# From the last differential head on, SyncE's transfers in written order, with strips and output weights moved and two casts reordered

## The chip, the cores and the metric

The kernel runs on one core of a Trainium2 chip. The metric is the device time of one execution in microseconds, taken as the median of several runs. Before the change the median is 902.08 us (three runs, 901.36 to 903.22).

## The reference: what is computed

One macaron block over 512 tokens of width 1024, in float32: half a SwiGLU feed-forward layer, a token mixer, another half feed-forward layer, a final RMS norm. The mixer is where the change lies. It has four differential heads (two softmax maps each, the second subtracted with a weight lambda, then an RMS norm of the head's output) and eight dilated heads. Cut to what matters:

```python
proj = h @ w_in
qa, ka, va, qb, kb, vb = jnp.split(proj, [...], axis=-1)
# 4 differential heads
s = q_blk @ k.T * scale + bias          # causal, -inf above the diagonal
p = softmax(s); a = p[0] - lam * p[1]
oa = rmsnorm(a @ v, subln_gain) * (1 - lam0)
# 8 dilated heads: three windows (128,1), (512,4), (2048,16), joined by their sums
ob = sum_over_windows(softmax-like weights) @ vb
mixed = concatenate([oa, ob])
x = x + mixed @ w_out
x = x + 0.5 * swiglu(rmsnorm(x, ffn2_norm), ...)
return rmsnorm(x, final_norm)
```

## The kernel before

All matrix products are done in a split form: each float32 operand is cast to a high part on ScalarE (ACT) and the remainder is formed on VectorE (DVE), and three products (high x high, high x low, low x high) are summed on TensorE (PE). So every weight tile needs a load (a DMA issued by SyncE, SP), a cast (line 1419, `high`) and a remainder (line 1423, `low`) before PE can use it.

**The steps.** The mixer is a list of chunks of matmuls, one per step; step 84 to 91 are the eight chunks of the query and key projection of the last unit (u = 7), steps 92 to 105 are the first fourteen chunks of the output projection (`wo_mm`, line 2067). The function `put(t, rank, f, ...)` (line 1391) adds an action to a step. `step(t)` (line 2100) sorts the actions of a step by rank, does those with a rank under 10, then the chunk, then the others. After that it takes one remainder from the list `lows` (line 2110; none in the step named by `held["hold"]`, two in the step behind that one), and one cast from the list `later`, whose remainder goes to `lows`.

**Who orders what.** PE runs in the order in which the instructions are written (`manual_schedule`, line 140). For DVE, ACT, GpSimd and SP in this stage, a list scheduler of the compiler decides the order; it starts from the written order and from its own estimate of when things are ready. The second feed-forward layer has SP and GpSimd in written order (line 1033).

**The units.** There are eight units u of attention, each with two maps m: u = 0 to 3 are the differential heads, u = 4 to 7 are pairs of dilated heads. For a row block i the function `score` (line 1740) has two matmuls into a PSUM bank of the tag "s" (two banks, used in turn), then a DVE instruction (line 1749) that adds the bias strip and takes the row's minimum, which frees the bank, then an exponential on ACT (line 1752). The strips (line 1169) are tiles of shifted bias rows, two for each unit, loaded by SP from a DRAM tile; units u and u - 2 share their slots.

**Turning the probabilities.** Products with the values need the probabilities transposed. Unit 7 and unit 4 do it on PE (`turn_part`, line 1865). Units 5 and 6 (6 in part) send them through DRAM: `flip` (line 1771) transposes 32 x 32 blocks on DVE; `away` (line 1778) writes the tile to the DRAM tile `pd` in four transfers of 160 KB on SP; `back` (line 1824) reads 640 KB of it into `ptx_dilated` in one transfer on SP, which must wait until all four have landed. Unit 5 does this for two halves, n = 1 and then n = 0. `values_moved` (line 1844) uses them on PE: its first 12 matmuls need half 1, the other 16 need half 0. It stands in step 97 for unit 5 and in step 101 for unit 6.

**The places that the change touches** (steps before the change):

- strips of unit 7: in `begin` (line 1732), at `put(s - 3, 0, begin)`, s = 97, so step 94
- `away` of unit 5: half 1 in step 87, half 0 in step 90; `back`: half 1 in step 89, half 0 in step 92
- `away` of unit 6, half 1: step 94; `back`: step 97
- output weights `wo_units[2]` (loaded by `ahead`, line 1436, in step 88), `[3]` (step 92), `[4]` (step 94), `[5]` (step 103, rank 10)
- `held["hold"]`: step 96
- `casts_q` of unit 6 (line 1636, two casts out of the PSUM bank of the queries): step 84, rank 9; `finish_low` of unit 2 (line 1979, the remainder of that head's output, which frees the bank "t" that its transposes were in): step 85, rank 8. `finish` of unit 2 (line 1964) is in step 85, rank 3.
- the projected queries and keys of unit 7 are split by `evac_now` (line 1668), one half in step 93 and the other in step 94, rank 8

A raw weight tile has three buffers, so a weight load can start only when the remainders of the weight three before it are formed.

Of the kernel before, what the change touches and what calls it, by code (L numbers as in the profile page):

```python
# [40 lines left out]
DIFF_FLIP = (11, 7)  # L41
DIFF_BACK = (16, 12)
DIFF_TAKEN = 21
DIFF_SETTLE = (20, 16)
OWN_SLOTS = (22, 23, 24)
PART_PLACES = {(0, 0): 0, (1, 0): 2560, (0, 1): 512, (1, 1): 896, (0, 2): 1280, (1, 2): 1664}
# [88 lines left out]
def tile_macaron(ctx: ExitStack, tc, xs, xT, wf, wgu1, wst1, wdg1, wqk, wvd, wo, wgu2, wst2,  # L135
# [1253 lines left out]
    at = {}  # L1389

    def put(t, rank, f, *a):
        at.setdefault(t, []).append((rank, f, a))

    units, chunks = [], []
    held = {}
# [207 lines left out]
    def qk_chunks(u):  # L1603
        us = [unit(wqk[u, hf], f"qk{u}{hf}") for hf in range(2)] if u > 1 else []
        st = qk_st[u] = {}

        def chunk(k):
            if k == 0:
                st["pq"] = mm_bank(f"pq{u}")
                st["pk"] = mm_bank(f"pk{u}")  # L1610
            if k % 4 == 0:
                ahead(us[k // 4])
            wh, wl = ready[us[k // 4]]
            for c, pt in ((0, st["pq"]), (1, st["pk"])):
                o = (k % 4) * 256 + c * P
                mm3(pt[:], wh[:, o:o + P], wl[:, o:o + P], xh[k][:], xl[k][:],
                    k == 0, k == KD - 1)
        def tiles():
            b0 = 31 + (u % 2) * 6
            qk[u] = [slot(b0 + i, f"{n}{u}", F32R)  # L1620
                     for i, n in enumerate(("q0", "q1", "k0", "k1", "l0", "l1"))]
            return qk[u]

        def cast_q(o, a):
            A.activation(o, a, AF.Copy, scale=-(HD ** -0.5))

        def rest_q(o, a, h):
            V.scalar_tensor_tensor(o, a, -(HD ** -0.5), h.bitcast(F32), op0=ALU.mult, op1=ALU.subtract)

        def casts_k():  # L1630
            _, _, k0, k1, _, _ = qk[u]
            pk = st["pk"]
            cast(k0[lo, :], pk[lo, :])
            cast(k1[hi, :], pk[hi, :])

        def casts_q():
            q0, q1, _, _, _, _ = qk[u]
            pq = st["pq"]
            cast_q(q0[lo, :], pq[lo, :])
            cast_q(q1[hi, :], pq[hi, :])  # L1640

        def evac_k():
            q0, q1, k0, k1, l0, l1 = qk[u]
            pk = st["pk"]

            def other_half(t, a, b):
                nc.sync.dma_start(t[b, :].bitcast(F32), t[a, :].bitcast(F32))

            other_half(k0, lo, hi)
            other_half(k1, hi, lo)  # L1650
            for a, b, kx, lx in ((lo, hi, k0, l0), (hi, lo, k1, l1)):
                rest(lx[a, :], pk[a, :], kx[a, :])
                other_half(lx, a, b)

        def rests_q():
            q0, q1, _, _, _, _ = qk[u]
            pq = st["pq"]
            for a, b, qx in ((lo, hi, q0), (hi, lo, q1)):
                rest_q(qx[b, :], pq[a, :], qx[a, :])

        def taken():
            tiles()
            for n, i, f in (("pq", 28, -(HD ** -0.5)), ("pk", 30, 1.0)):
                t = slot(i, f"{n}c{u}")[:]
                V.tensor_scalar_mul(t, st[n][:], f)
                st[n] = t

        def evac_now(first):

            if first and u < 2:  # L1670
                tiles()
            q0, q1, k0, k1, l0, l1 = qk[u]
            pq, pk = st["pq"], st["pk"]
            a, b, qx, kx, lx = (lo, hi, q0, k0, l0) if first else (hi, lo, q1, k1, l1)
            if u > 1:
                cast(qx[a, :], pq[a, :])
                rest(qx[b, :], pq[a, :], qx[a, :])
            else:
                cast_q(qx[a, :], pq[a, :])
                rest_q(qx[b, :], pq[a, :], qx[a, :])  # L1680
            cast(kx[a, :], pk[a, :])
            cast(kx[b, :], pk[a, :])
            rest(lx[a, :], pk[a, :], kx[a, :])
            A.copy(lx[b, :], lx[a, :].bitcast(F32))

        e = early_end[u] if u < 2 else start[f"q{u}"] + 7
        if u in DIRECT:
            put(e, 11, taken)
            put(e + 2, 8, evac_now, True)
            put(e + 3, 8, evac_now, False)  # L1690
        else:
            put(e, 11, tiles)
            put(e + 1, 2.5, casts_k)
            put(e + 1, 9, casts_q)
            put(e + 1, 11, evac_k)
            put(e + 2, 9, rests_q)
        if u < 2:
            return [lambda c=c: early_chunk(c) for c in range(8 * u, 8 * u + 8)]
        return [lambda k=k: chunk(k) for k in range(KD)]
# [17 lines left out]
    def attention(u, s):  # L1717
        diff, quick, moved = u < 4, u == 7, u in MOVED
        st = {}
        order = (1, 2, 0, 3) if u >= PAIRED_ROWS or u in MOVED_DIFF else range(NQ)  # L1720

        def row(m, i):
# [6 lines left out]
            o = m * 640 + (0, 0, 2 * P, P)[i]  # L1729
            return st["pr"][i in (1, 2)][:, o:o + w]  # L1730

        def begin():
            st["b"] = [strip(2 * u + m, (u % 2) * 2 + m) for m in range(2)]
            st["pr"] = [tp.tile([P, 1280], F32, tag=f"pr{m}", name=f"pr{u}{m}") for m in range(2)]
            for n in ("mx", "ls", "rl"):
                st[n] = sp.tile([P, 2, NQ], F32, tag=n, name=f"{n}{u}")
            for n in ("cc", "cs", "ss"):
                st[n] = sp.tile([P, NQ], F32, tag=n, name=f"{n}{u}")
# [247 lines left out]

        put(s - 3, 0, begin)
        if quick:
            held["hold"] = s - 1
        step = 1 if quick else 2  # L1990
        for n, i in enumerate(order):
            for m in range(2):
# [4 lines left out]
        if diff:  # L1997

            step, tv = 2 if u else 1, s + (DIFF_TAKEN if u in MOVED_DIFF else 13)
            if u in MOVED_DIFF:  # L2000
                for n in range(2):
                    put(s + DIFF_FLIP[n], 9.2, diff_flip, n)
                    put(s + DIFF_FLIP[n], 9.3, diff_away, n)
                    put(s + DIFF_BACK[n], 2, diff_back, n)
                    put(s + DIFF_SETTLE[n] - (n == 0), (9.5, 1.5)[n], settle, n)
                put(tv + (u == 0), 1, diff_values)
            else:
                put(tv - 2 - step, 2, turn, ((0, 2), (1,)))
                put(tv - 2, 2, turn, ((3,),))
                put(tv, 1, values)  # L2010
            e = tv + 1
            put(e, 7, squares)
            put(e + 1, 7, mean)
            put(e + 3, 5, scale)
            put(e + 6 - (u == 3), 3, finish)
            put(e + 7 - (u > 1), 8 if u < 3 else 1, finish_low)
        elif quick:

            for j, part in enumerate((((0, 0, 3),), ((1, 1, 3), (2, 2, 3)),
                                      tuple((k, 3, 4) for k in range(NQ)))):  # L2020
                for m in range(2):
                    put(s + 4 + j, 2, turn_part, m, part)
            put(s + 7, 1, values_part, tuple((k, k, NQ) for k in range(NQ)))
            put(s + 7, 3, finish)
            put(s + 7, 4, finish_low)
        elif moved:
            put(s + 6, 7, flip, 1)
            put(s + 6, 7.1, away, 1)
            put(s + BACK[u], 2, back, 1)
            if 0 in MOVED[u]:  # L2030
                put(s + 9 + (u == 4), 9 if u == 4 else 5, flip, 0)
                put(s + 9 + (u == 4), 9.1 if u == 4 else 5.1, away, 0)
                put(s + 11 + (u == 4), 2, back, 0)
            else:
                for n, part in enumerate((((0, 0), (1, 0)), ((0, 3),), ((1, 3),))):
                    put(s + 10 + n, 2, turn_rows, part)
            tv = s + TAKEN[u]
            put(tv, 1, values_moved)
            put(tv + 1, 3, finish)
            put(tv + 1, 8, finish_low)  # L2040
        else:
            tv = s + 9
            late = 2 * (u == 4)
            parts = ((0, 0, 4),), ((1, 1, 4),), ((2, 2, 4), (3, 3, 4))
            for j, part in enumerate(parts):
                for m in range(2):
                    put(tv + j + late * (1 + (j == 2)) // 2, 2, turn_part, m, part)
                put(tv + 4 + late, 1, values_part, part)
            put(tv + 5 + late, 3, finish)
            put(tv + 5 + late, 8, finish_low)  # L2050

    for w in plan:
# [3 lines left out]
        u = int(w[1])  # L2056
# [3 lines left out]
    wo_units = [unit(wo[n], f"wo{n}") for n in range(KD)]  # L2060
# [20 lines left out]
    chunks += [lambda kp=kp: wo_mm(0, 3, (2 * kp, 2 * kp + 1)) for kp in range(3)]  # L2081
    chunks += [lambda tt=tt: [wo_mm(0, t, (KD - 2,)) for t in (tt, tt + 1)] for tt in (0, 2)]
    put(wo_start, 0, prep, wo_units[2])
    put(wo_start, 0, load, wo_units[3])
    put(wo_start + 2, 0, load, wo_units[4])
    put(wo_start + 9, 10, prep, wo_units[3])
    put(wo_start + 11, 10, prep, wo_units[4])
    put(wo_start + 11, 10, load, wo_units[5])
# [27 lines left out]
            lows.append(lo_)  # L2116

    seam(step)
    for t in range(16, max(len(chunks), max(at) + 1)):
        step(t)  # L2120
    assert not later
    for f in lows:
        f()
# [237 lines left out]
```

## Time and profile before

| what | value |
|---|---|
| median of three runs | 902.08 us |
| the profiled execution | 904.04 us |
| its span, first to last instruction | 902.30 us |
| mean granted TensorE clock | 0.997 |
| PE busy | 891.2 us (99%) |
| DVE busy | 755.1 us (84%) |
| ACT busy | 569.9 us (63%) |
| GpSimd busy | 118.3 us (13%) |
| DMA, mean over the span | 175 GB/s |

The profiled execution lies 1.96 us above the median, and its span lies 1.74 us below its own time. All durations below are from this one execution. Lines of the profile name an engine, the line of the kernel (L1855 is line 1855), the operation, and `out<-in` by the names of the tiles with buffer numbers left out. SPq is SyncE's queue of DMA issues; PEld is the loading of weights into TensorE. In a list of waits the columns are the total in us, the count, and the longest. In a timeline they are the start, the duration, the operation and how often it stands there, and in square brackets the idle time before it with what ended it.

### The profile page before, as it was taken

The page shows a single profiled execution, that of the slowest core. Times are in us where ns is not written, and L with a number is a line of the kernel's source. Part 1 is how long each engine was busy: PE and PEld are TensorE (multiplying, and loading weights), DVE is VectorE, ACT ScalarE, POOL GpSimd, SP SyncE. Part 2 cuts the span into 40 slices and gives each one's busy share as a digit, 9 for nine tenths or more (in the row PEclk, how much of TensorE's full clock was granted, in tenths as well). Part 3 has the DMA queues.
Part 4 walks back from the last instruction along what each step waited for, and adds up shares of the span by engine and source line. Part 5 has one row for each costly group of instructions (what it writes and reads, how often), then busy time and mean ns, then how long its engine had stood idle before and what let it go on. Part 6 is the DMA issues. An engine that isn't in the chain of part 4 may idle for free.

```text
span 902.3 us, 15911 instructions
## 1 busy us (share of the span) xinstructions
PE 891.2 (99%) x5600; PEld 801.4 (89%) x5600; DVE 755.1 (84%) x1523; ACT 569.9 (63%) x1211; POOL 118.3 (13%) x148
## 2 busy tenths in 40 slices
PE   9999999999999999999999999999999999999997
PEld 7888998899999889887887778989999889999885
DVE  7698998889888888889996845888888888988985
ACT  7355765466667766766888765656665646666573
POOL 0100202121122110100000000111111112212200
PEclk9999999999999999999999999999999999999999
DMA  7464869678788762635675613466779679779902
GB/s 258 128 157 125 212 197 256 140 200 187 189 216 272 203 182 82 159 99 161 207 200 196 204 52 114 101 180 151 168 189 248 163 173 256 200 179 239 253 28 94
DMA packets 79665, 158.31 MB, mean 175 GB/s; under 512 B 9121, under 2 KB 15265, under 8 KB 79585
## 3 DMA queue, kind: packets, MB, share of 16 engines
q1 hardware_dynamic: 62000, 125.09, 43.2%
q0 software_dynamic: 17584, 32.20, 22.0%
q8 instruction: 44, 0.72, 0.3%
q14 instruction: 37, 0.30, 0.1%
HBM read 146.86 MB, written 6.73 MB: 170 GB/s over the span
## 4 chain that ended last, share of the span: by engine, by line
PE 92%; ACT 3%; DVE 2%; DMA 2%; issue 1%; SPq 0%; POOLq 0%; DVEq 0%; ACTq 0%
PE pt L197 8%; PE pt L195 8%; PE pt L196 8%; PE pua L196 2%; PE pua L195 2%; PE pua L197 2%; PE pwo L195 1%; PE pwo L196 1%; PE pwo L197 1%; PE pga L195 1%; PE pga L196 1%; PE pga L197 1%; PE pq L195 1%; PE pygb L195 1%; PE pygb L196 1%; PE pygb L197 1%
## 5 line engine op out<-in xcount | busy, mean ns | idle before, releaser
L1752 ACT ACTIVATE pr<-pr,mx 128x256 f32<-128x256 f32 (+3 forms) x64 | 36.0, 563 | 25.3 <-DVE mx L1749 24.5
L551 DVE SCALAR_TENSOR_TENSOR x<-pt,x 128x512 f32<-128x512 f32 x50 | 33.2, 689 | 17.2 <-PE pt L197 11.9
L1749 DVE CUSTOM_DVE_ANT_0 pr<-sc,strip 128x256 f32<-128x256 f32 (+3 forms) x64 | 30.7, 484 | 5.8 <-PE sc L1747 5.2
L453 ACT CAST w<-raa 128x512 fp32r<-128x512 f32 x34 | 20.9, 622 | 19.1 <-DVE raa L421 11.2
L457 DVE TENSOR_TENSOR w<-s2b,w 128x512 fp32r<-128x512 f32 x38 | 26.1, 686 | 8.0 <-ACT w L453 8.0
L453 ACT CAST w<-rab 128x512 fp32r<-128x512 f32 x28 | 17.3, 622 | 18.4 <-DVE rab L421 10.1
L453 ACT CAST w<-s2b 128x512 fp32r<-128x512 f32 x38 | 23.6, 620 | 6.9 <-DVE s2b L426 6.9
L195 PE MATMUL pwo<-w,mh 128*128 128x512 f32 x64 | 26.3, 410 | 0.0
L196 PE MATMUL pwo<-w,mh 128*128 128x512 f32 x64 | 25.3, 396 | 0.0
L197 PE MATMUL pwo<-w,ml 128*128 128x512 f32 x64 | 25.3, 395 | 0.0
L457 DVE TENSOR_TENSOR w<-s2a,w 128x512 fp32r<-128x512 f32 x30 | 20.6, 686 | 3.0 <-ACT w L453 2.9
L453 ACT CAST w<-s2a 128x512 fp32r<-128x512 f32 x30 | 18.6, 621 | 6.6 <-DVE s2a L426 5.8
L457 DVE TENSOR_TENSOR w<-raa,w 128x512 fp32r<-128x512 f32 x34 | 22.7, 685 | 0.0
L196 PE MATMUL pxgb<-ttb,w 128*128 128x256 f32 x80 | 22.5, 281 | 0.0
L1746 PE MATMUL sc<-k,q 128*128 128x256 f32 (+3 forms) x64 | 21.4, 336 | 0.8 <-DVE mx L1749 0.8
L396 POOL DMA_DIRECT2D s1bg<-wst_dram x10 | 8.7, 874 | 93.7 <-DVE w L457 39.7
L228 POOL TENSOR_TENSOR yi<-ss,half 128x4 f32<-128x4 f32 x4 | 4.1, 1016 | 127.7 <-DVE ss L1954 91.9
L1747 PE MATMUL sc<-l,q 128*128 128x256 f32 (+3 forms) x64 | 20.7, 325 | 0.0
L196 PE MATMUL pxub<-ttb,w 128*128 128x256 f32 x72 | 20.2, 281 | 0.0
L228 POOL TENSOR_TENSOR fin<-fin,half 128x1 f32<-128x1 f32 (+1 forms) x7 | 4.0, 569 | 117.6 <-DVE fin L1293 68.4
L396 POOL DMA_DIRECT2D s1ag<-wst_dram x8 | 7.1, 888 | 93.6 <-DMA s1ag<-wst_dram 38.1
L457 DVE TENSOR_TENSOR w<-rab,w 128x512 fp32r<-128x512 f32 x28 | 18.8, 685 | 0.3 <-ACT w L453 0.2
(1176 smaller groups left out, 3932.3 us busy)
## 6 DMA issues: line engine op xcount, KB each, us to landing
raw_qk<-wqk_dram SPq DMA_DIRECT2D x12, 512.0 KB, 3.7
raw0bg<-wst_dram SPq DMA_DIRECT2D x10, 512.0 KB, 5.2
raw0bu<-wst_dram SPq DMA_DIRECT2D x9, 512.0 KB, 5.9
raw_gua<-wgu_dram SPq DMA_DIRECT2D x8, 512.0 KB, 3.5
raw0ag<-wst_dram SPq DMA_DIRECT2D x8, 512.0 KB, 4.9
strip<-bias_rows SPq DMA_DIRECT2D x16, 256.0 KB, 4.0
raw_wo<-wo_dram SPq DMA_DIRECT2D x8, 512.0 KB, 4.1
raw0au<-wst_dram SPq DMA_DIRECT2D x7, 512.0 KB, 6.1
```

Of the source, the lines that this page charges most:

```text
L195: T.matmul(po, wh, mh, start=first, stop=False, skip_group_check=on)
L196: T.matmul(po, wh, ml, start=False, stop=False, skip_group_check=on)
L197: T.matmul(po, wl, mh, start=False, stop=last, skip_group_check=on)
L228: G.tensor_tensor(y, v, half[:, :v.shape[-1]], op=ALU.pow)
L396: nc.gpsimd.dma_start(t[:], b, accum_op=ALU.add)
L453: A.copy(made[t][0], source(t))
L457: V.tensor_tensor(l, source(t), h.bitcast(F32), op=ALU.subtract)
L551: V.scalar_tensor_tensor(o, a, f, b, op0=ALU.mult, op1=op1)
L1746: T.matmul(ps[:, :w], qs[:, qi], ks[:, :w], start=True, stop=False)
L1747: T.matmul(ps[:, :w], qs[:, qi], ls[:, :w], start=False, stop=True)
L1749: V.tensor_tensor_reduce(out=pi, in0=ps[:, :w], in1=st["b"][m][:, w - 1::-1], op0=ALU.add, op1=ALU.min, scale=1.0, scalar=3.0e38, accum_ou ...
L1752: A.activation(pi, pi, AF.Exp, scale=-1.0, bias=st["mx"][:, m, i:i + 1], accum_out=st["ls"][:, m, i:i + 1])
```

## The change

The last part of the stage, from step 86 on, is put under a region in which SP issues its transfers in written order. To make that order, the loads of strips and output weights are given other steps, and two small actions and the held step are moved:

- `strips` of unit 7 leave `begin` and go to step 89, rank 0.5, ahead of `back` of unit 5's half 1 (rank 2)
- `wo_units[2]` is loaded in step 86, `[3]` in step 90 (rank 3, ahead of `away` of half 0 with rank 5.1), `[4]` in step 94, rank 3 (ahead of `away` of unit 6 with rank 7.1); `[5]` keeps step 103 and so comes after `back` of unit 6
- the held step is 94 instead of 96
- `casts_q` of unit 6 goes from step 84, rank 9, to step 85, rank 3.2; `finish_low` of unit 2 from step 85, rank 8, to step 85, rank 3.1

From step 86 the written order of SP is then: output weight 2; `away` of unit 5, half 1 (four); strip, strip; `back`, half 1; output weight 3; `away`, half 0 (four); `back`, half 0; output weight 4; `away` of unit 6 (four); `back` of unit 6; output weight 5.

```diff
+QUEUE_ORDERED = 86
...
             put(e, 11, tiles)
             put(e + 1, 2.5, casts_k)
-            put(e + 1, 9, casts_q)
+            put(e + 1 + (u == 6), 3.2 if u == 6 else 9, casts_q)
...
+        def strips():
+            st["b"] = [strip(2 * u + m, (u % 2) * 2 + m) for m in range(2)]
+
         def begin():
-            st["b"] = [strip(2 * u + m, (u % 2) * 2 + m) for m in range(2)]
+            if "b" not in st:
+                strips()
...
         put(s - 3, 0, begin)
         if quick:
-            held["hold"] = s - 1
+            put(s - 8, 0.5, strips)
+            held["hold"] = s - 3
...
-            put(e + 7 - (u > 1), 8 if u < 3 else 1, finish_low)
+            put(e + 7 - (u > 1), 3.1 if u == 2 else 8 if u < 3 else 1, finish_low)
...
     put(wo_start, 0, prep, wo_units[2])
-    put(wo_start, 0, load, wo_units[3])
-    put(wo_start + 2, 0, load, wo_units[4])
+    put(wo_start - 6, 0, load, wo_units[2])
+    put(wo_start - 2, 3, load, wo_units[3])
+    put(wo_start + 2, 3, load, wo_units[4])
...
     seam(step)
-    for t in range(16, max(len(chunks), max(at) + 1)):
+    for t in range(16, QUEUE_ORDERED):
         step(t)
+    with tc.manual_schedule(engines={mybir.EngineType.SP}):
+        for t in range(QUEUE_ORDERED, max(len(chunks), max(at) + 1)):
+            step(t)
```

## The prediction

> **What bounds the kernel now.** I read the busy shares of the page first, then the list of PE's waits, the chain of waits around the longest of them, the clock by stretches, and the timelines of PE, DVE, ACT and SP there.
>
> ```profile
> PE 891.2 (99%) x5600; PEld 801.4 (89%) x5600; DVE 755.1 (84%) x1523; ACT 569.9 (63%) x1211; POOL 118.3 (13%) x148
> ```
>
> PE is busy 891.2 us of a span of 902.3, so no order of transfers can bring more than the 11 us in which PE stands still, plus what a standstill costs afterwards. The list of PE's waits tells which of those are in reach.
>
> ```profile
> core 0 of [0], span 902.3 us
> PE po L1855 <- DMA ptx_dilated<-pd: 2.2, 1, 2.2
> ...
> PE pt L1872 <- DVE ml L1982: 0.4, 1, 0.4
> ```
>
> The wait of 2.2 us is in the stage of the change: `values_moved` of unit 5 waits for `back` of half 0. The 0.4 us behind line 1982 is `finish_low`, also edited. The two entries left out lie at the kernel's start and long ahead of step 84; neither is touched. The chain of waits shows what the longest wait hangs on (start, duration, what):
>
> ```profile
> 503.69 6.49 DMA pd<-tr
> ...
> 510.26 3.91 DMA ptx_dilated<-pd
> ```
>
> The last quarter of `away` is issued at 503.69 and takes 6.49 us to land; only then can `back` go, 3.91 us more, to 514.17. The stretches show the price on PE (stretch, its length, PE busy, granted clock, DMA share, GB/s):
>
> ```profile
> 505.00:510.00 5.00, 5.00 (x24) 1.00 0.95 320
> 510.00:514.00 4.00, 2.02 (x16) 1.00 0.69 220
> 514.00:519.00 5.00, 4.78 (x27) 0.66 0.85 232
> ```
>
> Behind the standstill the clock is 0.66 on the mean of 5 us, where it was 1.00. That is 5 x 0.34 = 1.70 us lost beside the wait itself. The wait and its echo thus cost 2.2 + 1.7 = 3.9 us.
>
> The Trainium skill, TensorE: Matmul & The Clock Gate, Part 1, has the clock go to half only after an idle window of about 3.4 us and come back after as long a busy one. By that rule a pause of 2.2 us would have cost no clock, and removing it would bring 1.7 us less. The trace disagrees on the trigger, with the 0.66 right behind a pause of 2.2 us; the length lost fits half a clock for 3.4 us.
>
> **The change part by part.**
>
> *The order on SP.* Before, the scheduler had this order:
>
> ```profile
> 495.48 1.34 SPq L1782 DMA_DIRECT2D pd<-tr  x2
> ...
> 501.46 0.30 SPq L1782 DMA_DIRECT2D pd<-tr  x1
> 502.33 0.34 SPq L1827 DMA_DIRECT2D ptx_dilated<-pd  x1
> 502.72 1.42 SPq L1782 DMA_DIRECT2D pd<-tr  x3
> 504.18 0.49 SPq L1172 DMA_DIRECT2D strip<-bias_rows  x1
> 504.72 0.99 SPq L1408 DMA_DIRECT2D raw_wo<-wo_dram  x1
> pd<-tr SPq DMA_DIRECT2D x4, 160.0 KB, 2.8
> ```
>
> The `back` of half 1 stood behind the first quarter of `away` of half 0, which had to wait for its flip until 501.46. So 640 KB of reading back started at 502.33, just ahead of the other three quarters, with a strip and an output weight on their heels: the engines are 0.95 busy from 505 to 510. In the new order `back` of half 1 no longer waits for that flip. `away` of half 1 ends its issues at 496.8; its quarters took 2.8 us (last row, transfers issued between 490 and 500 us). The two strips go out behind it; their slots are free by then, with unit 5's last reduction at 495.52 (in a fence below). So `back` of half 1 is issued at about 499.7 instead of 502.33, output weight 3 right after it. Behind that waiting `back` stand only this weight and `away` of half 0, whose flip ends later anyway, so the wait holds up nobody.
>
> *When does half 0 come?* By their shapes 524 kB of strips, 655 kB of `back`, 524 kB of weight and 655 kB of `away` pass from 496.8 on, 2.36 MB. At 320 GB/s that is 7.4 us, at 232 GB/s 10.2 us: the queue is through between 504.2 and 507.0. The quarters themselves cannot be issued before the flip: 501.46 less the 0.36 of the next part, four issues of 0.45 us, so 502.9, plus 2.8 is 505.7. I take 506.5 for the landing; the bounds are 505.7 and 502.9 + 6.49 = 509.4. Then `back` of half 0 lands 3.91 later, at 510.4 (bounds 509.6 and 513.3), instead of 514.17.
>
> The Trainium skill, DMA: Bandwidth & Descriptors, Queues, rings and completion order, speaks against the change here: each DMA engine takes its queue in order and marks a transfer as done only after all its earlier writes, so strips and a weight put ahead of `away` delay it. The trace agrees: the quarter with a `back` ahead of it took 6.49 us, those of half 1 took 2.8. By that rule alone the late bound, 513.3, would be the value to take, and the time that of the late half among the rivals.
>
> *The two casts.*
>
> ```profile
> 484.37 1.20 ACT L1625 ACTIVATE q<-pq 64x512 fp32r<-64x512 f32 x2
> ...
> 486.95 0.69 ACT L1974 ACTIVATE mh<-ot,sub 128x512 fp32r<-128x512 f32 x1
> ...
> 513.51 0.62 ACT L1684 CAST l<-l 64x512 fp32r<-64x512 f32 x1 [0.32 <-DVE l L1195]
> ...
> 530.64 0.62 ACT L1419 CAST w<-raw_wo 128x512 fp32r<-128x512 f32 x1
> ```
>
> `casts_q` (1.20 us on ACT) now stands behind `finish` (the row at 486.95) instead of ahead of it. So the cast and the remainder behind it, which frees the bank that PE waits for, come about 1.2 us earlier, more than the wait of 0.36 us in the next fence. That wait goes: 0.36 us. The query remainders, which follow `casts_q`, still end before step 88, where unit 6 first needs them.
>
> ```profile
> 488.57 0.52 PE L1872 MATMUL pt<-ident,pr 128*128 128x128 f32 x3 [0.36 <-DVE ml L1982]
> ...
> 510.72 1.30 PE L1855 MATMUL po<-ptx_dilated,v 128*64 128x256 f32 x12
> ...
> 526.37 2.39 PE L1855 MATMUL po<-ptx_dilated,v 128*64 128x256 f32 x28
> ```
>
> *What is late next.* PE reaches `values_moved` of unit 5 at 510.72 - 0.36 = 510.36. Its second part starts 1.30 us later, at 511.66, and half 0 is there at 510.4. Unit 6 does the same 28 matmuls in 2.39 us at full clock (last row), so PE is through at 512.75. Then come the first two scores of unit 7, map 0 and map 1. Each is a pair of matmuls of 256 columns, and 12 of that width took 1.30 us (row at 510.72), so a pair takes 0.22 and map 1 is wanted at 512.97. Here DVE is behind:
>
> ```profile
> 495.52 0.69 DVE L1749 CUSTOM_DVE_ANT_0 pr<-sc,strip 128x512 f32<-128x512 f32 x1 [0.93 <-PE sc L1747]
> ...
> 507.94 0.69 DVE L1195 TENSOR_TENSOR q<-pqc,q 64x512 fp32r<-64x512 f32 x1 [1.07 <-ACT q L1192]
> ...
> 510.48 1.56 DVE L1776 STREAM_TRANSPOSE tr<-pr 128x640 f32<-128x640 f32 x2
> ...
> 513.51 0.69 DVE L1423 TENSOR_TENSOR w<-raw_wo,w 128x512 fp32r<-128x512 f32 x1
> 514.12 0.68 DVE L1749 CUSTOM_DVE_ANT_0 pr<-sc,strip 128x512 f32<-128x512 f32 x1
> ```
>
> DVE last waits for PE at 495.52; from there it has its own chain with ACT up to the last row, so it moves with PE's 0.36 us and no more. Two things hold the score of map 1: the bank, freed by the reduction at 514.12 to 514.80, and unit 7's last key remainder, copied by ACT from 513.51 to 514.13. The standstill of before hid both. The held step now lets the remainder of line 1423, in the row at 513.51, go behind that reduction: the reduction starts where the remainder did, at 513.51 - 0.36 = 513.15, and ends at 513.83; the copy ends at 513.77. So the score waits from 512.97 to about 513.85, 0.9 us. That is the new wait in the place of the old. One step on, DVE still owes the moved remainder (0.69) and unit 6's normalisations before it frees the banks for the next scores; I charge 0.5 us, between 0 (it catches up) and 0.9.
>
> *The other loads.* Output weight 2 stands first in the new order, ahead of `away` of half 1, which waits for its flip anyway. Output weights 3 and 4 go out later than before, at about 500 and 507, but the first cast of weight 3 is the row at 530.64; weight 5 goes behind unit 6's `back` and is cast later still. I cost these at nothing; if that cover were gone, a late weight would stop PE microsecond for microsecond. `back` of unit 6 now has no weight ahead of it but `away`, and is wanted only in step 101.
>
> *The sum.* Removed: 2.2 (DMA wait) + 1.7 (clock) + 0.36 (bank) = 4.26. Added: 0.9 + 0.5 = 1.4. The sum is 2.86 us, with no new fall of the clock. The profiled execution would go from 904.04 to 901.2. It lies 1.96 above the median, which goes from 902.08 to 899.2. With the added waits at both their ends (0 and 1.8) this case spans 897.8 to 899.6.
>
> **The rivals.** About 0.2%, or 1.8 us, is what a measurement of this kernel can tell from no change.
>
> *The clock falls again.* The remaining pause of 0.9 us, with 0.5 behind it, starts another stretch at half clock. For it: 2.2 us did. Against: the pause of 0.36 us had none, as its stretch shows.
>
> ```profile
> 484.00:490.00 6.00, 5.64 (x41) 1.00 0.38 87
> ```
>
> It costs 1.7, of which 0.5 would hide the second wait, so 1.2: 900.4. The Trainium skill, TensorE: Matmul & The Clock Gate, Part 1, would have no fall after a pause under its 3.4 us; the stretch at 0.66 speaks against leaning on that.
>
> *Half 0 still comes late.* The traffic put ahead of `away` keeps it near the late bound, 513.3. PE then waits 1.6 us instead of 2.2, the clock falls as before, and DVE's lag is hidden again. The gain is 514.17 - 513.3 = 0.87, plus the bank's 0.36: 900.9.
>
> *The order is written but PE's time is not made by it.* DVE or ACT are placed otherwise by the scheduler, because its own estimates have changed, and lose on the flips what the queue gains: 902.1.
>
> *Slower.* The same queue, but at a lower rate: strips read shifted copies of one row, and in front of `away` they hold everything up. It decides from the point at which half 0 lands after 514.2, that is when the 2.36 MB are not through by 510.3, under 175 GB/s. The rows above have 220 to 320 under load, which speaks against it. At 130 GB/s they are through at 515.0, half 0 comes at 518.9, 4.7 us later, and the time is 906.4 after the 0.36.
>
> **How the numbers follow.** The forecast gets 0.55, the clock's fall 0.18, the late half 0.10, no effect 0.10, the slower queue 0.07. The predicted time is the first, 899.2. The range goes from 897.4 (this case's low end, with 0.4 for the scatter of medians) to 902.3, which takes in the first three rivals and leaves out the slower queue and the edges. Faster by over 0.2% means below 900.28: nearly all of the forecast and half of the clock's case, 0.62. Within 0.2%: the rest of that, the late half, most of no effect, 0.29. Slower: 0.09.
>
> **What would show it.** Right: in the waits of PE the 2.2 us for `ptx_dilated` and the 0.4 us for line 1982 are gone; `back` of half 1 is issued near 499.7 and lands well before 510; `back` of half 0 is issued near 506.5; the stretch of 514 to 519 has a clock near 1.00; a wait of about 0.9 us for DVE line 1749 or ACT line 1684 appears at unit 7's second score. Wrong: `po` still waits for DMA; the clock still shows 0.66 there; the quarters of half 0 land after 509.4; or PE waits for an output weight.

## The result, and the profile after

The changed kernel takes 900.40 us (median of 22 runs, 899.85 to 902.83), the kernel before 902.23 us (22 runs beside them, 900.96 to 904.47). The ratio is 0.9977, 95% interval 0.9970 to 0.9984: 1.4 to 2.7 us faster. The prediction said 899.2, in a range of 897.4 to 902.3. The profiled execution of the changed kernel took 900.48 us, with a span of 898.7.

Lines behind the edits have moved: line 1855 of before (`values_moved`) is 1860, line 1749 (the reduction) 1754, line 1782 (`away`) 1787, line 1827 (`back`) 1832, line 1684 (the key's copy on ACT) 1685, line 1756 (the reciprocal behind the reduction) 1761, line 1982 (`finish_low`) 1987.

The list of PE's waits of the changed kernel (total us, count, longest):

```profile
core 0 of [0], span 898.7 us
engine line waited for: us in total, times, longest us
...
PE sc L1751 <- DVE mx L1754: 0.8, 2, 0.4
PE sc L1751 <- DVE rl L1761: 0.8, 1, 0.8
```

The 2.2 us for `ptx_dilated` and the 0.4 us for line 1982 are gone. The last line is the wait that the prediction put in their place. The line above it is no new one: it stands in the kernel before too, 0.8 us in two pieces. The profile names the reciprocal of line 1761 and neither the reduction nor the copy; that it is the wait meant is read from the rows of DVE and ACT, where the reduction and the copy both end just ahead of the score at 513.50:

```profile
512.65 0.69 DVE L1754 CUSTOM_DVE_ANT_0 pr<-sc,strip 128x512 f32<-128x512 f32 x1
...
513.27 0.16 DVE L1761 RECIPROCAL rl<-ls 128x2 f32<-128x2 f32 x1
```

```profile
512.65 0.62 ACT L1685 CAST l<-l 64x512 fp32r<-64x512 f32 x1 [0.32 <-DVE l L1196]
```

The same three stretches as before (length, PE busy, granted clock, DMA share, GB/s):

```profile
505.00:510.00 5.00, 5.00 (x24) 1.00 0.46 139
510.00:514.00 4.00, 3.19 (x33) 1.00 0.79 248
514.00:519.00 5.00, 5.00 (x28) 1.00 0.69 224
```

The clock stays at 1.00 where it was 0.66, and the crowd of transfers at 505 to 510 has gone from 0.95 to 0.46. SP's timeline shows why; two answers on the landing times follow it (issues at 500.5 to 503 us, and at 507 us):

```profile
493.28 1.76 SPq L1787 DMA_DIRECT2D pd<-tr  x4
495.09 1.11 SPq L1173 DMA_DIRECT2D strip<-bias_rows  x2
497.41 0.32 SPq L1832 DMA_DIRECT2D ptx_dilated<-pd  x1
498.08 0.33 SPq L1409 DMA_DIRECT2D raw_wo<-wo_dram  x1
500.61 2.16 SPq L1787 DMA_DIRECT2D pd<-tr  x4
506.91 0.34 SPq L1832 DMA_DIRECT2D ptx_dilated<-pd  x1
507.36 0.37 SPq L1409 DMA_DIRECT2D raw_wo<-wo_dram  x1
```

```profile
pd<-tr SPq DMA_DIRECT2D x4, 160.0 KB, 4.9
```

```profile
ptx_dilated<-pd SPq DMA_DIRECT2D x1, 640.0 KB, 3.7
```

`back` of half 1 goes out at 497.41, before the flip of half 0 (DVE has it at 499.01), and no longer behind a quarter of `away`. `back` of half 0 goes out at 506.91 and lands 3.7 us later, at 510.6. PE's timeline says when that is needed:

```profile
487.43 0.82 PE L1877 MATMUL pt<-ident,pr 128*128 128x128 f32 x6
...
509.87 2.39 PE L1860 MATMUL po<-ptx_dilated,v 128*64 128x256 f32 x28
...
513.50 0.36 PE L1751 MATMUL sc<-k,q 128*128 128x256 f32 x1 [0.81 <-DVE rl L1761]
...
522.83 2.39 PE L1860 MATMUL po<-ptx_dilated,v 128*64 128x256 f32 x28
```

The 28 matmuls of unit 5's `values_moved` run without a break. Half 0 is needed 1.30 us after 509.87, at 511.17, so it comes with 0.56 us to spare. The six transposes at 487.43 stand together where before the bank's wait split them.

For the experiments I compare one length that lies within PE's timeline: the **stage**, from the start of unit 3's products (485.20 in the changed kernel, 485.49 before) to the start of unit 6's `values_moved` (522.83, last row, and 526.37 before). It is 37.63 us, and was 40.88. What is left of the span is 861.1 and 861.4, so nearly all of the profiled pair's gain lies in the stage.

### The profile page after: what moved, and what is told of

Read it like the earlier page. It is cut to its first block, busy times and chain, and to the rows that moved or that the text cites. A ratio compares the mean times of both kernels' runs of the same rounds, so it can differ in the third digit from the quotient of the medians.

```text
span 898.7 us, 15910 instructions
## 1 busy us (share of the span) xinstructions
PE 888.7 (99%) x5600; PEld 799.7 (89%) x5600; DVE 753.8 (84%) x1523; ACT 569.6 (63%) x1211; POOL 118.2 (13%) x148
## 4 chain that ended last, share of the span: by engine, by line
PE 95%; DVE 3%; ACT 1%; issue 1%; DMA 0%; POOLq 0%; DVEq 0%; SPq 0%; ACTq 0%
PE pt L197 8%; PE pt L198 8%; PE pt L196 8%; PE pua L197 2%; PE pua L196 2%; PE pua L198 2%; PE pwo L196 1%; PE pwo L198 1%; PE pwo L197 1%; PE pq L196 1%; PE pq L197 1%; PE pq L198 1%; PE pk L196 1%; PE pk L197 1%; PE pk L198 1%; PE pga L196 1%
```

## The experiments

The runs of a kernel stand beside runs of the kernel before on the same chip; these have a median of 902.86 beside e1 to e4, 903.45 beside e5 to e7 and 902.10 beside e8 to e11, so that medians of different groups are not compared more closely than that. The ratios hardly separate kernels whose stages differ by less than 1 us: such differences are read from one profiled execution of each. "Pause" is what PE's timeline gives as idle time in the stage; "clock down" counts the executions whose mean granted clock over the whole span is 0.997 or less, where the others show 0.998 or 0.999.

| kernel | median us | ratio to before, 95% | stage us | pauses in the stage, us | clock down |
|---|---|---|---|---|---|
| before, profiled | 902.23 | | 40.88 | 0.36 bank, 2.19 half 0 | 30 of 93 |
| e1_again (before) | 902.01 | 0.9988 to 1.0008 | 39.23 | 0.36 bank, 2.06 half 0 | 4 of 12 |
| e2_order_only | 901.67 | 0.9980 to 1.0002 | 38.59 | 0.36 bank, 0.55 half 0, 0.65 score | 0 of 12 |
| e3_casts_only | 901.66 | 0.9989 to 1.0010 | 38.15 | 1.55 half 0 | 1 of 12 |
| e4_written_only | 901.46 | 0.9980 to 1.0000 | 38.59 | 0.36 bank, 1.11 score | 0 of 12 |
| e5_moves_only | 906.86 | 1.0035 to 1.0062 | 43.86 | 5.35 half 0 | 5 of 5 |
| e6_no_hold | 900.88 | 0.9972 to 0.9993 | 38.03 | 1.42 score | 0 of 12 |
| changed kernel | 900.40 | 0.9970 to 0.9984 | 37.63 | 0.81 score | 0 of 22 |
| e7_late_prep | 900.64 | 0.9974 to 0.9994 | 37.46 | 0.24 score, 0.34 next score | 0 of 12 |
| e8_unmoved | 900.47 | 0.9974 to 0.9992 | 37.63 | 0.60 half 0 | 0 of 11 |
| e9_flip_behind | 901.66 | 0.9988 to 1.0005 | 39.11 | 0.81 score, 1.43 next score | 0 of 11 |
| e10_flip_and_prep | 901.51 | 0.9981 to 0.9998 | 38.54 | 0.25 score, 1.43 next score | 0 of 11 |
| e11_early_values | 905.19 | 1.0018 to 1.0043 | 41.44 | 0.36 bank, 2.71 half 0 | 10 of 12 |

The 30 of 93 for the kernel before are its runs beside the experiments. In most kernels a few executions are 2 to 3 us longer without a lower clock (in the kernel before on one chip 9 of 35, at 903.46 to 904.79); the profiled one of e2_order_only is such a one (903.11), and its stage begins later (486.87) while it is not longer, so that loss lies ahead of the stage. Its cause stays open.

### The kernel before once more

No edit.

> The kernel before, unchanged, run again so that the single executions can be looked at with their clocks. Theory A: the wait for half 0 (2.2 us) is there in every execution, but the fall of the clock behind it (1.7 us in the profile of before) only in some, so the times fall into two groups about 1.7 to 2 us apart, and the longer ones have the lower mean clock (0.997 against 0.998 to 0.999). Rival: the clock falls in every execution and the longer ones come from a longer wait for the transfer; then the mean clock is the same in short and long ones.

Measured: the wait for half 0 is there again, and the clock does not fall. The waits and the stretch behind the pause:

```profile
PE po L1855 <- DMA ptx_dilated<-pd: 2.1, 1, 2.1
```

```profile
514.00:519.00 5.00, 5.00 (x36) 1.00 0.85 241
```

Of the 12 executions eight take 901.49 to 902.27 at a mean clock of 0.998 or 0.999, four take 903.09 to 903.76 at 0.997. So the stage with the fall to 0.66 is 1.65 us longer than the one without (40.88 less 39.23). About 0.13 of that is the longer wait (2.19 against 2.06), which leaves some 1.5 for the fall; the prediction had 1.70. But it comes only in some executions: in all, in 34 of the 105 listed of the kernel before. The execution profiled for the prediction, with a mean clock of 0.997, was of that kind.

### The queue's order without the casts and the held step

```diff
-            put(e + 1 + (u == 6), 3.2 if u == 6 else 9, casts_q)
+            put(e + 1, 9, casts_q)
...
-            held["hold"] = s - 3
+            held["hold"] = s - 1
...
-            put(e + 7 - (u > 1), 3.1 if u == 2 else 8 if u < 3 else 1, finish_low)
+            put(e + 7 - (u > 1), 8 if u < 3 else 1, finish_low)
```

> The change without the two reordered casts and without the earlier held step: only SyncE's order and the moved loads. Theory: the wait of 2.2 us for half 0 goes; the wait of 0.36 us for the bank of unit 2 stays; unit 7's second score waits longer than in the changed kernel, 0.8 + 0.6 = 1.4 us, because a remainder of 0.69 us now stands ahead of the reduction. Gain on before without the clock 2.2 - 1.4 = 0.8 us, with the clock 0.8 plus up to 1.7: ratio about 0.998. Rival: the order of the transfers is all of the gain, and the ratio is that of the whole change, 0.9977, with a second score that waits 0.8 us.

Measured: the stage is 0.64 shorter than that of the kernel before without a fall of the clock (39.23 to 38.59). PE still waits 0.55 for half 0, and 0.65 appears at the second score, so 1.20 of the 2.06 stays under two names. The order does not deliver the whole alone. The second score starts 29.47 us after unit 3's products (486.87 to 516.34), and e4_written_only, where PE does not wait for half 0 at all, has it at 29.46: in both its start is set by DVE and ACT, not by half 0.

```profile
516.34 0.36 PE L1751 MATMUL sc<-k,q 128*128 128x256 f32 x1 [0.65 <-DVE rl L1761]
```

### The casts alone

```diff
-            put(e + 1, 9, casts_q)
+            put(e + 1 + (u == 6), 3.2 if u == 6 else 9, casts_q)
...
-            put(e + 7 - (u > 1), 8 if u < 3 else 1, finish_low)
+            put(e + 7 - (u > 1), 3.1 if u == 2 else 8 if u < 3 else 1, finish_low)
```

> The kernel before with the two reordered casts alone. Theory: the wait of 0.36 us for unit 2's bank goes, with 0.2 us of restart; flips and transfers come earlier by the same, so the wait for half 0 stays at 2.2 us and the time goes down by 0.4 to 0.6 us, ratio 0.9994. Rival: PE only reaches half 0 earlier and waits there so much longer (2.6 to 2.8 us), ratio 1.0000.

```profile
PE po L1855 <- DMA ptx_dilated<-pd: 1.5, 1, 1.5
```

Measured: the bank's wait goes, and the wait for half 0 does not grow by it but shrinks by 0.5. Counted from unit 3's products, PE reaches half 0 and DVE's flip of it starts 0.55 us earlier than in e1_again, both alike, which would leave the wait as it was; `back` is issued 1.04 earlier (23.71 against 24.75), so the quarters of half 0 also land half a microsecond sooner. Why they do is open. The stage is 1.08 shorter than in e1_again, more than the order brings alone. The two do not add up: order and casts together, without the held step (e6_no_hold), bring 1.20.

### The written order alone

```diff
+QUEUE_ORDERED = 86
...
-    for t in range(16, max(len(chunks), max(at) + 1)):
+    for t in range(16, QUEUE_ORDERED):
         step(t)
+    with tc.manual_schedule(engines={mybir.EngineType.SP}):
+        for t in range(QUEUE_ORDERED, max(len(chunks), max(at) + 1)):
+            step(t)
```

> The kernel before with SyncE in written order from step 86 on, and nothing moved: output weight 2 behind away of half 1, output weight 3 ahead of back of half 0, the strips behind it. Theory: what matters is that back of half 1 no longer stands behind the first quarter of away of half 0; half 0 lands by about 510 and the time is that of the order-only kernel, ratio 0.998. Rival: the moves are needed, because output weight 3 now competes with half 0; then half 0 lands at 512 or later and a wait for it of 1 us or more remains, ratio 0.999 to 1.000.

```profile
PE sc L1747 <- DVE rl L1757: 1.1, 1, 1.1
```

Measured: with strips and weights where they were, the written order takes away the whole wait for half 0; the second score waits 1.11 instead (at 515.15, 29.46 us after unit 3's products at 485.69). The stage is 38.59, the same as with the moved loads in e2_order_only, where the wait for half 0 was 0.55. The moves add nothing to the order.

### The moved loads in the scheduler's order

The changed kernel without the region (the diff above, taken back).

> The whole change without the region of written order: loads, casts and held step are moved, and the scheduler orders SyncE. It then puts back of half 1 behind the first quarter of away of half 0 as before, and back of half 0 behind the first quarter of away of unit 6, which waits for a flip that ends near 511. Theory: half 0 is issued only near 511.5 and lands near 515, PE waits for it 3 to 4 us, and the time is 1 to 2 us above before, ratio 1.001 to 1.002. Rival: the moved steps are what helps, ratio 0.998.

Measured: 0.5% slower. The wait and its place are as expected, but it is 5.35 us, not 3 to 4. The waits, SP's timeline and the stretch behind the pause:

```profile
PE po L1860 <- DMA ptx_dilated<-pd: 5.4, 1, 5.4
```

```profile
501.35 0.34 SPq L1832 DMA_DIRECT2D ptx_dilated<-pd  x1
...
511.42 0.30 SPq L1787 DMA_DIRECT2D pd<-tr  x1
511.89 0.34 SPq L1832 DMA_DIRECT2D ptx_dilated<-pd  x1
```

```profile
514.00:519.00 5.00, 2.29 (x16) 0.50 0.84 308
```

Now the scheduler puts the first quarter of unit 6's `away`, which must wait for its flip until 511.42, ahead of `back` of unit 5's half 0. It is the fault of the kernel before, a waiting transfer ahead of a ready one, in a second place. So these edits are safe only under a written order; which of them (loads, casts or held step) leads the scheduler to it was not separated.

### The held step taken back

```diff
-            held["hold"] = s - 3
+            held["hold"] = s - 1
```

> The changed kernel with the held step back at 96. Theory: a remainder of 0.69 us stands again ahead of the reduction that frees the bank, so unit 7's second score waits 0.8 + 0.6 = 1.4 us and the time is 0.6 us above the changed kernel, about 901.0 where that has 900.4. Rival: the score waits for the copy of the key remainder on ScalarE, not for the reduction, and the held step changes nothing.

Measured: the second score waits 1.42 instead of 0.81, and the stage is 38.03, 0.40 longer. The held step is worth 0.4 us of the stage, less than the 0.61 of the wait; where the rest goes is told further down. The times (900.88 and 900.40) do not separate the two kernels.

### Output weight 2 three steps later

```diff
-    put(wo_start, 0, prep, wo_units[2])
+    put(wo_start + 3, 0, prep, wo_units[2])
```

> The changed kernel with the casts and remainders of output weight 2 put off by three steps, so that VectorE has one remainder of 0.69 us less ahead of unit 7's key remainder and the reduction. Theory: VectorE's lag is what unit 7's second score waits for; it comes 0.6 us earlier, its wait goes from 0.8 to about 0.2 us, and the time is 0.6 us below the changed kernel. Rival: the wait is bound by ScalarE's chain, and stays at 0.8 us; or the late remainders stop the output projection at step 98, which would show as a wait of PE for line 1424.

```profile
512.53 0.36 PE L1751 MATMUL sc<-k,q 128*128 128x256 f32 x1 [0.24 <-DVE rl L1761]
514.95 0.44 PE L1751 MATMUL sc<-k,q 128*128 128x384 f32 x1 [0.34 <-DVE mx L1754]
```

Measured: with the weight's cast and remainder out of the way the wait falls from 0.81 to 0.24, as expected, and 0.34 of it comes back one score on. The stage is 0.17 shorter, which the time does not show. The wait is work that ACT and DVE have to do before unit 7's scores; moved, it is met again.

### The moved loads taken back, the order kept

```diff
-            put(s - 8, 0.5, strips)
...
-    put(wo_start - 6, 0, load, wo_units[2])
-    put(wo_start - 2, 3, load, wo_units[3])
-    put(wo_start + 2, 3, load, wo_units[4])
+    put(wo_start, 0, load, wo_units[3])
+    put(wo_start + 2, 0, load, wo_units[4])
```

> The changed kernel, but with the strips and the loads of output weights where the kernel before puts them: the written order, the two casts and the held step stay. Theory: what helps is that SyncE's order is written out, not that strips and weight 2 are moved ahead of the transfers of half 1. Half 0 lands in time, the second score of unit 7 waits some 0.8 us for DVE, the stage from unit 3's products to unit 6's values_moved takes 37.6 us within 0.3, and the time is that of the changed kernel, ratio 0.998 to the kernel before. Rival: output weight 3, now ahead of the way back of half 0, makes PE wait 0.5 us or more for half 0, and the stage takes 38.1 or more.

Measured: stage and time are those of the changed kernel (37.63; 900.47 against 900.40), as the theory had it, but not in its way: PE waits 0.60 for half 0, as the rival said, and then hardly for the second score. Its PE timeline, the issue of output weight 3, and the landing times for issues from 500 to 503 and at 505.25:

```profile
511.37 1.31 PE L1856 MATMUL po<-ptx_dilated,v 128*64 128x256 f32 x16 [0.60 <-DMA ptx_dilated<-pd]
```

```profile
502.21 0.50 SPq L1409 DMA_DIRECT2D raw_wo<-wo_dram  x1
```

```profile
pd<-tr SPq DMA_DIRECT2D x4, 160.0 KB, 3.2
raw_wo<-wo_dram SPq DMA_DIRECT2D x1, 512.0 KB, 5.0
```

```profile
ptx_dilated<-pd SPq DMA_DIRECT2D x1, 640.0 KB, 6.1
```

Without strips and a weight ahead of them the quarters of half 0 land in 3.2 us instead of 4.9; but now `back` takes 6.1 instead of 3.7. When it is issued at 505.25, weight 3 ahead of it is still on its way (issued at 502.21, 5.0 us, so until about 507.2), and strips and weight 4 follow right behind; the changed kernel's `back` had nothing in flight ahead of it (0 GB/s from 506.8 to 507.2) and one weight behind. So what goes first decides which of the two transfers pays. The Trainium skill, DMA: Bandwidth & Descriptors, Queues, rings and completion order, has each DMA engine take its queue in order; the quarters and `back` both agree with it. Whether the transfers behind `back` cost it anything too is not shown. And whether PE waits for half 0 or a moment later for DVE is the same here.

### The flip behind the reduction

```diff
-            put(s + 6, 7, flip, 1)
-            put(s + 6, 7.1, away, 1)
+            put(s + 6 + (u == 6), 7, flip, 1)
+            put(s + 6 + (u == 6), 7.1, away, 1)
```

> The changed kernel with unit 6's first flip and its way out one step later, so that unit 7's second reduction need not stand behind 1.56 us of transposes on DVE. Theory: the 0.81 us wait of unit 7's second score is only DVE's order. It goes, and with it 0.6 to 0.8 us of the stage (37.63 to about 36.9); time 0.7 us below the changed kernel, about 899.7. Rival: the wait only moves, to a later score or to the products of unit 6's turned half, whose way back now starts later; the stage stays at 37.4 or more.

```profile
510.56 0.69 DVE L1196 TENSOR_TENSOR q<-pqc,q 64x512 fp32r<-64x512 f32 x1 [1.51 <-ACT q L1193]
...
513.21 1.56 DVE L1781 STREAM_TRANSPOSE tr<-pr 128x640 f32<-128x640 f32 x2
```

```profile
512.84 0.35 PE L1751 MATMUL sc<-k,q 128*128 128x256 f32 x1 [0.81 <-DVE rl L1761]
...
516.34 0.44 PE L1751 MATMUL sc<-k,q 128*128 128x384 f32 x1 [1.43 <-DVE mx L1754]
```

Measured: the theory falls. The wait of 0.81 stays, and 1.43 is added; the stage is 39.11, 1.5 us longer. In the first fence (DVE) the place of the two transposes is now an idle time of 1.51 us in which DVE waits for ACT's cast of the query: in the changed kernel the flip cost nothing there. So the second score does not hang on DVE's flip; DVE's remainders, its reduction and the score all hang on ACT's casts of unit 7's queries and keys. ACT comes to these at 509.91, behind an exponential (509.08) that needs DVE's reduction before it (508.36 to 509.04): the two engines take turns. At 513.21 the flip holds up the next reductions.

### Flip and output weight 2, both later

Both diffs above.

> As the run with the flip behind the reduction, and output weight 2's cast and remainder three steps later as well. Theory: DVE then owes nothing between unit 7's reductions; no wait of PE over 0.2 us is left in the stage, which takes 36.8 us; time about 899.6, ratio 0.997 to the kernel before. Rival: a new wait of 0.5 us or more takes the place (the late weight, the way back of unit 6, or the casts that crowd behind), and the time is no better than that of the changed kernel, 900.4.

Measured: the first wait falls to 0.25 as in e7_late_prep, the 1.43 of e9_flip_behind stays; stage 38.54. The rival holds: no better than the changed kernel, and worse by the flip.

### A longer pause in the kernel before

```diff
-TAKEN = {5: 16, 6: 13}
+TAKEN = {5: 15, 6: 13}
```

> The kernel before with unit 5's values_moved one step earlier; nothing of SyncE's queue is changed. PE reaches half 0 about 1.4 us sooner and so stands still for 3.4 to 3.7 us instead of 2.2; what it would have done after is done after the pause, so that the pause alone costs about 1.4 us. Theory: the chance of the clock's fall grows with the pause's length. It was in 21 of 70 executions of the kernel before at 2.2 us and in 5 of 5 at 5.4; here it should be in clearly more than 30%, at least 7 of 12, and the typical time 903 to 905. Rival: the fall comes by chance that has nothing to do with the pause's length, and about 4 of 12 executions show a mean clock of 0.997 or less.

The waits and the stretch behind the pause:

```profile
PE po L1855 <- DMA ptx_dilated<-pd: 2.7, 1, 2.7
```

```profile
514.00:519.00 5.00, 5.00 (x24) 0.66 0.92 252
```

Measured: the pause is 2.71 in the profiled execution, less than the 3.4 to 3.7 expected, since half 0 came earlier too. Ten of 12 executions show a mean clock of 0.997 or less, against 13 of 35 of the kernel before on the same chip. The rival, a chance that has nothing to do with the pause, falls. The median, 905.19, lies just above the 903 to 905 expected. Four executions show 0.995, with 905.87 to 908.35 us; whether their clock fell for longer or once more is open.

## Why the prediction was right, and where it was off

**The order on SP: right.** `back` of half 1 was to go out at about 499.7; it went at 497.41, since the last quarter of half 1 was out before 495.09 and not at 496.8. Half 0 was to be back in DRAM at 506.5 and to land in SBUF at 510.4; `back` was issued at 506.91 and landed at 510.6. e4_written_only shows that the order is the cause. The moved strips and weights, which the prediction counted as part of this order, add nothing to it: e8_unmoved does as well without. Nor is the last half microsecond of half 0 worth anything: in e8_unmoved it came 0.60 late and the stage was the same, because the second score is bound by DVE and ACT.

**The wait in its place: right.** 0.9 us was charged for unit 7's second score, 0.81 came. Its ground was half right: the reduction and the copy were named, but what both hang on is ACT's casts (e9_flip_behind, e7_late_prep).

**The bank's wait: somewhat more than charged.** It was 0.36; to the start of unit 5's `values_moved`, counted from unit 3's products, the changed kernel needs 24.67 us (485.20 to 509.87) and the kernel before 25.23 (485.49 to 510.72), 0.56 less. Splitting the six transposes had cost 0.2 beside the wait.

**The next step's wait: smaller than charged.** 0.5 us was charged, between 0 and 0.9, for DVE still being behind with the moved remainder. The list of waits has nothing, but the timeline shows 0.2: one score on, PE starts 0.34 us behind the start of the two transposes ahead of it, just as DVE's reduction ends (515.48), where the kernel before without a fall (e1_again, second fence) needs 0.14.

```profile
515.20 0.38 PE L1842 MATMUL pt<-ident,pr 128*128 128x128 f32 x2
515.54 0.44 PE L1751 MATMUL sc<-k,q 128*128 128x384 f32 x1
```

```profile
516.70 0.38 PE L1837 MATMUL pt<-ident,pr 128*128 128x128 f32 x2
516.84 0.42 PE L1746 MATMUL sc<-k,q 128*128 128x384 f32 x1
```

In e6_no_hold, where the remainder is not moved, it is 0.13. So the held step saves 0.61 of the first wait and gives back 0.2 at the next.

**The clock: the term that was mis-sized.** The step that was wrong is "It lies 1.96 above the median, which goes from 902.08 to 899.2". The profiled execution went from 904.04 to 900.48, 3.56 us, even more than the 2.86 of the sum. But it lay above the median *because* its clock had fallen, and the sum took the 1.70 for that fall off the median as well, where two executions out of three have no fall. Weighted by 34 of 105, the 1.65 between the two stages becomes 0.32 x 1.65 = 0.53. With the stage's 1.60 (39.23 to 37.63, no fall in either) that makes 2.1 us in the mean; the ratio gives 902.23 x 0.0023 = 2.1 (the two medians alone 1.83). The prediction's other terms without the clock, 2.2 + 0.36 - 1.4 = 1.16, were 0.4 too low for the stage, which hid a part of the error. That 900.40 lies in the range says little by itself: the range was wide enough for no effect at all, 902.1. The list of waits and the clock are what bear the account out.

**Where the 1.60 comes from:** the casts, the written order and the held step. From e1_again over e2_order_only and e6_no_hold to the changed kernel: the order 0.64, the casts behind it 0.56, the held step 0.40. The other way about, over e3_casts_only, the casts bring 1.08 and the order 0.12 behind them. The waits agree: 2.06 + 0.56 - 0.81 = 1.81, less the 0.2 at the next score. What bounds the steps of this path is the second score's start, counted from unit 3's products: 29.47 us in e2_order_only, 28.90 in e6_no_hold, 28.30 in the changed kernel.

**The rivals.** The clock did not fall in any of 22 executions. That rival had forecast 900.4, which is the time measured; this is a coincidence: its fall did not come, and the forecast was too low for the 1.70 that it took off the median. Half 0 was in time. The flips did not lose what the queue gained: the first quarter of half 0 was issued at 500.61, where it had been 501.46. The slower queue did not come either: half 0 landed at 510.6, not after 514.2. e5_moves_only is slower by its queue, yet not for a lower rate but for a waiting transfer at the head.

## What to carry to other kernels

Before a term of a profiled execution is subtracted from a median, ask whether the median has it: an execution 2 us above the median with a stretch at a low clock is the sign that it has not. In a queue taken in order, look for the transfer that waits for an engine while a ready one stands behind it; of all that was done to the queue here, only that mattered, and pulling other loads forward did nothing under the written order. A wait at the end of a chain of two engines that take turns does not go away by moving one link; ask first what that engine would do instead in the time.

## What the runs showed of the hardware

In this kernel a short standstill of PE lowers its clock by chance, and the chance grows with its length. By the longest pause of each kernel's profiled execution: up to 1.43 us, no execution of 103 with a mean clock of 0.997 or less; 1.55 us, one of 12; 2.06 to 2.19 us, 34 of 105; 2.71 us, 10 of 12; 5.35 us, five of five, these at 0.994 to 0.995. That the loss lies behind this pause is seen only in the profiled executions (0.66 before, 0.66 in e11_early_values, 0.50 in e5_moves_only, each over 514 to 519); of the others the mean alone is known. The Trainium skill, TensorE: Matmul & The Clock Gate, Part 1, lets the clock fall after an idle window of about 3.4 us, with windows that run freely. Chance that depends on where the pause falls in a free window agrees with the runs; a length of 3.4 us does not, as falls came after 2.2 and 2.7 us. An estimate from the counts: if a window must be idle as a whole, a share of 0.32 at 2.1 to 2.2 us would belong to a window of 1.6 to 1.7 us (2.15 / 1.32), which would also have 0.6 to 0.7 at 2.71 (10 of 12 came) and none below it (the one of 12 at 1.55 does not fit, unless that execution's pause was longer); no run measures the window itself.
